# A decoder layer in which the gated MLP's up projection becomes one level of Strassen's product and its down projection is summed in one piece

## The chip, the cores and the metric

The kernel runs on one core of a Trainium2 chip. The metric is the device time of one launch in microseconds. Three runs of the kernel before took 2831.7, 2834.8 and 2835.8 us. One further execution was taken by the hardware profiler, and every row below is from it.

## The reference, cut to what matters

One layer for 512 tokens of width 2048. Three mixers (sparse attention, a state-space scan, block attention) are gated and merged to `m`; the change does not touch them. Then:

```python
x = layer_norm(ALPHA * x + w_out(merged), ln1_g, ln1_b)          # x1, 512 x 2048
u = x1 @ w_up                                                    # 2048 -> 2 x 5632 (gate | value)
u = causal depthwise convolution of width 3 along the tokens, with bias
y = (gelu_tanh(u[:, :5632]) * u[:, 5632:]) @ w_down              # 5632 -> 2048
out = layer_norm(ALPHA * x1 + y, ln2_g, ln2_b)
```

All values are fp32. The kernel writes each operand as a high and a low part, v = h + l, and makes each product from three matmuls: h·h, h·l and l·h.

## The kernel before, in words

**Weights.** Blocks of 128 x 1024 values are loaded by SyncE (SP) into a ring `raw` of three buffers (`pair_unit` for the up projection, `load_raw` for the rest). `split_w` makes the high part `wh` on ScalarE (ACT, line 72) and the low part `wl` on VectorE (DVE, line 73), in rings of two buffers each. The scheduler gives these two a high priority, so in program order they stand early. Every engine works through its own list in order.

**Up projection.** `up_tile(j)`, for j in 0 to 43, takes 128 gate columns and the 128 value columns that go with them. The weights are the stationary operand, the 512 tokens move: 2 x 16 x 3 = 96 matmuls of 512 columns into two PSUM banks. For j = 0 each is cut in two halves of 256 tokens, 192 matmuls. `conv` then reads the bank three times: ACT makes one term (line 947), DVE adds two (line 949). ACT does the gelu, GpSimd (POOL) multiplies gate by value (line 970), and `split` makes `ah` and `al` (lines 83 and 85), which stay in SBUF.

**Down projection.** After every six tiles `down` multiplies the six activation tiles by their rows of `w_down`: four column groups of 512, four token tiles, a PSUM bank each from the side banks `atb` and `avb`. DVE adds each bank to `res` (line 991). The last group is done by `down_last`, token tile by token tile, with LayerNorm 2 behind each.

**LayerNorm 1 and its residual.** `norm_half` normalises two token tiles (line 904), transposes them on TensorE (PE) and applies gain and bias per partition while it writes the high and low parts of x1 (lines 912 to 917). `res` must become ALPHA · x1: `x1_scaled(t)` does this inside the first four up tiles with two POOL operations of 128x2048 (lines 936 and 937) and one ACT operation (line 938).

Of the kernel before, what the change touches and what calls it, by code (L numbers as in the profile page):

```python
# [9 lines left out]
F32 = mybir.dt.float32  # L10
# [21 lines left out]
# gates computed ahead after each part of the mixers  # L32
# [7 lines left out]
def tile_trunk(ctx: ExitStack, tc: tile.TileContext, x, rel_bias, w_in, cq_gain, ckv_gain,  # L40
# [54 lines left out]
    # W as the stationary operand: out[col tile] = W[:, cols]^T @ X^T, 512 tokens wide  # L95
# [16 lines left out]
    # 128 columns at the same place of both halves of a matrix's columns  # L112
# [37 lines left out]
    def s5_pow_e(pool, y, name):  # L150
        # e^y to the last bit or so: y = k ln2 + r, a polynomial in r, 2^k from the exponent bits
# [24 lines left out]
    lhsB = sp.tile([96, 4, 2, 4, P], F32R, name="lhsB")      # h, h, l; q, re/im, G, state  # L176
# [9 lines left out]
    def s5_params():  # L186
# [27 lines left out]
        # sine and cosine by half angles after reduction to [-pi, pi]  # L214
# [28 lines left out]
        # (lam_bar - 1) / lam  # L243
# [22 lines left out]
        # input matrices, block-diagonal over the two groups of a pair, inputs on partitions  # L266
# [27 lines left out]
        # output matrices with the states on partitions  # L294
# [12 lines left out]
        # e^{i theta t}, t < 32  # L307
# [112 lines left out]
    def logits(head, hd, qs, kst, mask):  # L420
        # normalised softmax rows of one head, the four query tiles side by side
# [62 lines left out]
    def u_split(G):  # L484
        # the stacked rows h, l, h of a pair of groups meet h, h, l of its matrices
# [8 lines left out]
    def s5_tile(G):  # L494
# [44 lines left out]
        # 2 gelu(y) in its tanh form  # L539
# [7 lines left out]
    def s5_glu():  # L547
        # 4 times the branch's output: (2 gelu) * (1 + tanh(z/2))
# [24 lines left out]
    def rms_apply(banks, gains, dst, width):  # L573
        # dst = c * gain * (mean(c^2) + eps)^-0.5; the mean token-major, then spread over the partitions
# [25 lines left out]
    def dsa_in():  # L600
# [6 lines left out]
        # index keys on both partition halves; index weights token-major  # L607
# [14 lines left out]
    # value at (p, m) stands for the distance p + 384 - m  # L622
# [26 lines left out]
    def dsa_topk():  # L649
        # exactly the 128 greatest scores of a row, the lower index first among equals  # L650
# [48 lines left out]
    def moba_v(g):  # L699
        # two token tiles share a bank: its flags are cleared once, by the first of them  # L700
# [120 lines left out]
    # merged (gates carried twice the sigmoid)  # L821
# [45 lines left out]

    CH = ((0, 512), (512, 512), (1024, 512), (1536, 256), (1792, 256))
    for c, (c0, n) in enumerate(CH):
        xt = xr.tile([P, NT, n], F32, tag="xt", name="xt")  # L870
        nc.sync.dma_start(xt, x2[:, c0:c0 + n].rearrange("(t p) n -> p t n", p=P))
        kq = 1024 // n
        if c < 4:
            banks = [mm_bank()[:, :n] for _ in range(NT)]
            for k0 in range(0, KD, kq):
                wh, wl = wunit(w_out[0], k0, kq, c0, n)
                for k in range(kq):
                    kk = k0 + k
                    for t in range(NT):
                        tok_mm(banks[t], t, mT[kk][0], mT[kk][1], wh[:, k], wl[:, k], kk == 0, kk == KD - 1)  # L880
# [11 lines left out]
        for ts in ((0,), (1,), (2, 3)):  # L892
            banks = [mm_bank()[:, :n] for _ in ts]
            for kk in range(KD):
                for t, bank in zip(ts, banks):
                    tok_mm(bank, t, mT[kk][0], mT[kk][1], *ws[kk], kk == 0, kk == KD - 1)
            for t, bank in zip(ts, banks):
                residual(t, c, c0, n, xt, bank)
    x1T = [(xp.tile([P, T], F32R, tag="x", name="x1h"), xp.tile([P, T], F32R, tag="x", name="x1l")) for _ in range(KD)]
    def norm_half(hb):  # L900
        hs = slice(256 * hb, 256 * hb + 256)
        for t in (2 * hb, 2 * hb + 1):
            mu, r_ = layer_norm_stats(t, 5)
# [184 lines left out]
```

## Time and profile before

| what | value |
|---|---|
| median of three runs | 2834.8 us (2831.7 to 2835.8) |
| span of the profiled execution | 2832.9 us |
| PE busy with matmuls | 2792.6 us, 99% |
| DVE, ACT, POOL busy | 1449.3, 889.5 and 224.5 us |
| last matmul starts | 2820.4 us |
| granted PE clock, stretch 1408 to 1428 us | 0.66 |

The span runs from the first to the last record of the profiled execution; the profiled execution's own time is this span, 1.9 us below the median of the runs. "Busy" of PE counts pipelined matmuls, so what one matmul costs is read from the distance between the starts of two of them, not from its own duration.

### The profile page before, as it was taken

To read this page: it belongs to the slowest core of one execution; us is meant where nothing else is said; L and a number is where in the kernel's file an instruction comes from. 1 tells how busy PE (TensorE), PEld (TensorE's weight loads), DVE (VectorE), ACT (ScalarE), POOL (GpSimd) and SP (SyncE) were. 2 spreads that over 40 slices of the span, in tenths; PEclk is the share of its full clock that TensorE was granted. 3 is DMA by queue.
4 is the path that set the end of the run, shared out by engine and by line. 5 is a ranking of instruction groups with operands and counts; after the bars stand their busy time and mean duration, and the time that the engine had idled before them with its cause. 6 is when DMAs were issued, how large, how long until landed. Compare 5 with 4: busy or idle time off the path is not lost.

```text
span 2832.9 us, 32264 instructions
## 1 busy us (share of the span) xinstructions
PE 2792.6 (99%) x12651; PEld 2255.8 (80%) x12655; DVE 1449.3 (51%) x2176; ACT 889.5 (31%) x1325; POOL 224.5 (8%) x163
## 2 busy tenths in 40 slices
PE   9999999999999999999899999999999999999998
PEld 7777877777887778889778888888888888888886
DVE  6357988885445446434553334333433333333448
ACT  3243333334344432212532232331322322322321
POOL 0000011110000003100420000000000000000002
PEclk9999999999999999999999999999999999999999
DMA  6223433334332335533433333333333333323333
GB/s 199 84 80 93 127 108 118 117 89 93 82 98 86 96 126 192 168 119 105 134 104 97 97 97 92 99 94 94 97 97 97 97 97 97 97 90 97 97 97 112
DMA packets 352824, 301.82 MB, mean 107 GB/s; under 512 B 20963, under 2 KB 307600, under 8 KB 352160
## 3 DMA queue, kind: packets, MB, share of 16 engines
q1 hardware_dynamic: 339536, 281.44, 33.2%
q10 hardware_dynamic: 10832, 14.12, 1.4%
q0 software_dynamic: 2304, 4.20, 0.6%
q8 instruction: 99, 1.62, 0.2%
q14 instruction: 53, 0.43, 0.0%
HBM read 278.31 MB, written 18.24 MB: 105 GB/s over the span
## 4 chain that ended last, share of the span: by engine, by line
PE 94%; DVE 3%; DMA 1%; issue 1%; POOL 1%; ACT 0%; DVEq 0%; SPq 0%; ACTq 0%; POOLq 0%
PE mmb L91 24%; PE mmb L93 23%; PE mmb L92 23%; PE atb L93 4%; PE atb L92 4%; PE atb L91 4%; PE avb L93 2%; PE avb L91 2%; PE avb L92 2%; PE atb L440 1%; PE atb L642 1%; PE atb L460 1%; PE mmb L711 1%; PE avb L536 1%; PE mmb L712 1%
## 5 line engine op out<-in xcount | busy, mean ns | idle before, releaser
L73 DVE TENSOR_TENSOR wl<-raw,wh 128x1024 fp32r<-128x1024 f32 (+1 forms) x468 | 601.1, 1285 | 946.6 <-ACT wh L72 930.2
L72 ACT ACTIVATE wh<-raw 128x1024 fp32r<-128x1024 f32 (+1 forms) x468 | 489.1, 1045 | 1364.1 <-PE mmb L92 905.0
L91 PE MATMUL mmb<-x1h,wh 128*128 128x512 f32 (+1 forms) x1440 | 552.7, 385 | 5.4 <-ACT wh L72 5.4
L92 PE MATMUL mmb<-x1l,wh 128*128 128x512 f32 (+1 forms) x1440 | 555.5, 386 | 1.6 <-DVE x1l L917 1.6
L93 PE MATMUL mmb<-x1h,wl 128*128 128x512 f32 (+1 forms) x1440 | 526.1, 385 | 6.8 <-DVE wl L73 6.8
L91 PE MATMUL mmb<-xh,wh 128*128 128x512 f32 (+1 forms) x1056 | 419.6, 398 | 1.2 <-ACT wh L72 1.2
L92 PE MATMUL mmb<-xl,wh 128*128 128x512 f32 (+1 forms) x1056 | 418.9, 397 | 0.0
L93 PE MATMUL mmb<-xh,wl 128*128 128x512 f32 (+1 forms) x1056 | 407.5, 397 | 0.6 <-DVE wl L73 0.6
L93 PEld LDWEIGHTS mmb<-x1h,wl 128*128 128x128 f32 x1440 | 270.9, 188 | 61.6 <-DVE wl L73 8.0
L91 PEld LDWEIGHTS mmb<-x1h,wh 128*128 128x128 f32 x1440 | 270.0, 188 | 60.0 <-ACT wh L72 6.3
L92 PEld LDWEIGHTS mmb<-x1l,wh 128*128 128x128 f32 x1440 | 271.3, 188 | 56.8 <-DVE x1l L917 2.6
L91 PEld LDWEIGHTS mmb<-xh,wh 128*128 128x128 f32 (+1 forms) x1056 | 199.3, 189 | 54.7 <-issue 9.0
L93 PEld LDWEIGHTS mmb<-xh,wl 128*128 128x128 f32 (+1 forms) x1056 | 198.7, 188 | 52.7 <-issue 9.4
L92 PEld LDWEIGHTS mmb<-xl,wh 128*128 128x128 f32 (+1 forms) x1056 | 199.1, 189 | 47.4 <-issue 6.9
L93 PE MATMUL atb<-wh,al 128*128 128x512 f32 x480 | 189.8, 395 | 0.0
L92 PE MATMUL atb<-wl,ah 128*128 128x512 f32 x480 | 189.5, 395 | 0.0
L949 DVE SCALAR_TENSOR_TENSOR cv<-mmb,cwc,cv 128x511 f32<-128x511 f32 (+1 forms) x176 | 131.6, 748 | 88.0 <-ACT cv L947 84.8
L91 PE MATMUL atb<-wh,ah 128*128 128x512 f32 x480 | 170.7, 395 | 0.0
L970 POOL TENSOR_TENSOR cv<-cv 128x512 f32<-128x512 f32 x44 | 57.7, 1311 | 1251.7 <-DVE cv L949 1251.7
L93 PEld LDWEIGHTS atb<-wh,al 128*128 128x128 f32 x480 | 89.9, 187 | 22.1
L91 PEld LDWEIGHTS atb<-wh,ah 128*128 128x128 f32 x480 | 90.0, 187 | 21.9
L92 PEld LDWEIGHTS atb<-wl,ah 128*128 128x128 f32 x480 | 90.0, 187 | 21.7
(369 smaller groups left out, 3342.6 us busy)
## 6 DMA issues: line engine op xcount, KB each, us to landing
raw<-in_w_up_dram SPq DMA_DIRECT2D x360, 256.0 KB, 3.4
raw<-in_w_in_dram SPq DMA_DIRECT2D x120, 512.0 KB, 3.7
raw<-in_w_down_dram SPq DMA_DIRECT2D x88, 512.0 KB, 3.6
raw<-in_w_out_dram SPq DMA_DIRECT2D x32, 512.0 KB, 3.7
raw<-in_w_branch_dram SPq DMA_DIRECT2D x24, 512.0 KB, 4.6
thd<-th ACTq DMA_DIRECT2D x22, 512.0 KB, 2.9
th<-thd SPq DMA_DIRECT2D x22, 512.0 KB
raw<-in_w_in_dram SPq DMA_DIRECT2D x32, 256.0 KB, 3.4
```

What stands on the lines that cost most here:

```text
L72: nc.scalar.activation(wh, raw, AF.Copy)
L73: nc.vector.tensor_sub(wl, raw, wh.bitcast(F32))
L91: nc.tensor.matmul(o, ah, bh, start=start, stop=False)
L92: nc.tensor.matmul(o, ah, bl, start=False, stop=False)
L93: nc.tensor.matmul(o, al, bh, start=False, stop=stop)
L440: nc.tensor.matmul(lb[:, :W], s[half, qi], kl[half, :W], start=False, stop=not mk)
L460: nc.tensor.transpose(tb[:, (i - j) * P:(i - j + 1) * P], pt[:, o:o + P], ident)
L536: nc.tensor.matmul(yb[rw], ctr[:, G, rw], t[0], start=True, stop=False, tile_position=(0, 32 * q))
L642: nc.tensor.matmul(lb[:, :W], qs[hd][half, qi], kil[half, :W], start=False, stop=True)
L711: nc.tensor.matmul(o, xh[:, ts_], wl[:, k], start=False, stop=False, skip_group_check=True)
L949: nc.vector.scalar_tensor_tensor(c_[:, s_:], bank[:, :T - s_], cwc[:, j * 88 + f:j * 88 + f + 1], c_[:, s_:], op0=ALU.mult, op1=ALU.add)
L970: nc.gpsimd.tensor_mul(ca, ca, cv)
```

## The change

**Up projection.** The 16 blocks of 128 that the sum runs over are taken as two halves of eight, the tokens as two blocks of 256, and gate and value columns as two column blocks, so one tile is a 2 x 2 block product. Strassen's product in Winograd's form needs seven block products in place of eight. `up_pair(j)` does them in this order on PE: w11·a11, t2·s2, t1·q1, w21·a12, t3·s3, t4·a22, w22·q4. Each is 8 x 3 = 24 matmuls of 256 columns. The token-side operands q1, s2, s3, q4 are built once, after LayerNorm 1. The weight-side sums t1 to t4 are built for each j: t1 and t3 on DVE, t2 and t4 on POOL (`wsum`, line 992), each 128x1024, in a pool `ts` of three buffers. The outputs are put together by DVE in SBUF (`u2`, `u3`, `hf1`, `hf2`, lines 1047 to 1057), and `conv` reads them from SBUF. The first two products of tiles 0 to 3 that need no sums (`pre`, `pre_end`) are done ahead.

**LayerNorm 1.** The last 256 columns of `w_out` are summed in two halves. `norm` applies gain and bias token-major with two DVE operations of 128x1024 for each half row, x1 is stored to DRAM (`resd`), and `turn` transposes 96 blocks, 64 before.

**Activations.** Each tile's product of gate and value is stored to DRAM (`actd`, line 1062, on ACT's queue).

**Down projection.** Two passes of 1024 output columns. In each, all 44 tiles are summed in eight PSUM banks. The activations are loaded again (line 1082, ACT's queue) and split again in each pass. x1 is loaded back (4 MB, line 1077), and `take` adds ALPHA · x1 to the banks at the end of a pass. In the second pass the last eight tiles are held, so that the token tiles end one after the other.

On DVE, a steady up tile before (`wl` is the low part of a weight block, `cv` the convolution, `al` the low part of an activation):

```order
L73 TENSOR_TENSOR wl<-raw,wh 128x1024 x2
L949 SCALAR_TENSOR_TENSOR cv<-mmb,cwc,cv 128x511
L949 SCALAR_TENSOR_TENSOR cv<-mmb,cwc,cv 128x510
L73 TENSOR_TENSOR wl<-raw,wh 128x1024
L949 SCALAR_TENSOR_TENSOR cv<-mmb,cwc,cv 128x511
L949 SCALAR_TENSOR_TENSOR cv<-mmb,cwc,cv 128x510
L73 TENSOR_TENSOR wl<-raw,wh 128x1024
L85 TENSOR_TENSOR al<-cv,ah 128x512
```

On DVE, the middle of a steady up tile of the change, from the split of w21 on (`ts` is t1 or t3, the two after it in a row are t3's and t4's low parts):

```order
L73 TENSOR_TENSOR wl<-raw,wh 128x1024
L992 TENSOR_TENSOR ts<-raw,raw_12905 128x1024
L73 TENSOR_TENSOR wl<-ts,wh 128x1024 x2
L992 TENSOR_TENSOR ts<-raw_12905,raw_12941 128x1024
L1050 TENSOR_TENSOR u_12829<-mmb,p_12671 128x256
L73 TENSOR_TENSOR wl<-raw_12702,wh 128x1024
L1052 TENSOR_TENSOR hf_12831<-mmb,u_12829 128x256
L1055 TENSOR_TENSOR hf_12672<-mmb,u_12829 128x256
L73 TENSOR_TENSOR wl<-raw,wh 128x1024
L1026 SCALAR_TENSOR_TENSOR cv<-hf_12672,cwc,cv 128x511
L1026 SCALAR_TENSOR_TENSOR cv<-hf_12672,cwc,cv 128x510
L1057 TENSOR_TENSOR hf_12831<-mmb,u_12799 128x256
```

Where a tile had four low parts, four convolution steps and one `al`, it now has seven low parts, two sums, five 256-wide operations and four convolution steps, and the convolution reads `hf` in SBUF where it read the bank `mmb`.

On POOL, two steady tiles of the change (`ts` is t2 or t4, `cv` the product of gate and value); before there was the `cv` row alone, line 970, once a tile:

```order
L992 TENSOR_TENSOR ts<-ts,raw_13180 128x1024
L1061 TENSOR_TENSOR cv<-cv 128x512
L992 TENSOR_TENSOR ts<-ts,raw 128x1024
L992 TENSOR_TENSOR ts<-ts,raw_13419 128x1024
L1061 TENSOR_TENSOR cv<-cv 128x512
L992 TENSOR_TENSOR ts<-ts,raw 128x1024
```

Two sums of 128x1024 a tile are new there, one ahead of the product and one behind it.

On ACT, from the last up tile to the first activations of the down projection in the change (`actd` is the store, `af` a load from it):

```order
L72 ACTIVATE wh<-raw 128x1024
L1024 ACTIVATE cv<-hf_21276,c_cb,cwc 128x512
L72 ACTIVATE wh<-raw 128x1024
L1024 ACTIVATE cv<-hf_21435,c_cb,cwc 128x512
L1060 ACTIVATE cv<-cv 128x512
L1062 DMA actd<-cv 128x512
L1082 DMA af<-actd 128x512 x4
L83 ACTIVATE ah<-af 128x512
L1082 DMA af<-actd 128x512
L83 ACTIVATE ah<-af 128x512
L1082 DMA af<-actd 128x512
```

What moved: the loads of all activation tiles stand behind the store of the last one, which waits for POOL's last product.

The core of the diff:

```diff
-    def up_tile(j):
...
-            banks = gemm_pair(wus, j, x1T)
-        ca = conv(banks[0], j)
-        cv = conv(banks[1], 44 + j)
+    def wsum(eng, a, b):
+        t_ = upl.tile([P, 8, P], F32, tag="ts", name="ts", bufs=3)
+        with tc.high_priority(HP):
+            eng.tensor_add(t_, a, b)
+        return t_
+    def prod(bank, src, name, first):
+        wh, wl = hl(src)
+        for k in range(8):
+            xh, xl = X[name, k]
+            for n, (a, b) in enumerate(((wh, xh), (wh, xl), (wl, xh))):
+                nc.tensor.matmul(bank, a[:, k], b, start=first and k == 0 and n == 0,
+                                 stop=k == 7 and n == 2, skip_group_check=True)
...
+    def up_pair(j, done):
+        w11, w12 = wblock(0, 0, j), wblock(0, 1, j)
+        t1 = wsum(nc.vector, w11, w12)
+        st = None if done else pre(j, w11, None)
+        w22 = wblock(1, 1, j)
+        t2 = wsum(nc.gpsimd, t1, w22)
+        B, C = chain_bank(j), chain_bank(j)
+        prod(B, t2, "s2", True)
+        prod(C, t1, "q1", True)
+        w21 = wblock(1, 0, j)
...
+        t3 = wsum(nc.vector, w12, w22)
+        t4 = wsum(nc.gpsimd, t2, w21)
+        nc.vector.tensor_add(u2, B, p1)
+        prod(B, t3, "s3", False)
+        nc.vector.tensor_add(u3, B, p1)
+        nc.vector.tensor_sub(hf2[:, HI], C, u3)
+        prod(Dk, t4, "a22", True)
+        nc.vector.tensor_add(hf1[:, HI], Dk, u3)
+        prod(C, w22, "q4", False)
+        nc.vector.tensor_sub(hf2[:, LO], C, u2)
+        ca = conv(hf1, j)
+        cv = conv(hf2, 44 + j)
         nc.scalar.activation(ca, ca, AF.Gelu_apprx_tanh)
         nc.gpsimd.tensor_mul(ca, ca, cv)
-        h = dp.tile([P, T], F32R, tag="ah", name="ah", bufs=2 * GA)
-        l = dp.tile([P, T], F32R, tag="al", name="al", bufs=2 * GA)
-        split(h, l, ca)
-        return h, l
+        nc.scalar.dma_start(actd[j], ca)
...
-    def x1_scaled(t):
-        nc.gpsimd.tensor_mul(res[:, t], res[:, t], g1b)
-        nc.gpsimd.tensor_add(res[:, t], res[:, t], b1b)
-        nc.scalar.activation(res[:, t], res[:, t], AF.Copy, scale=ALPHA)
...
+    def norm(t, c):
+        nc.vector.scalar_tensor_tensor(y, y, mu, g1b[:, cs_], op0=ALU.subtract, op1=ALU.mult)
+        nc.vector.scalar_tensor_tensor(y, y, r_, b1b[:, cs_], op0=ALU.mult, op1=ALU.add)
+        nc.scalar.dma_start(resd[:, t, cs_], y)
...
+        block("a22", kk, xp, b22)
+        nc.vector.tensor_sub(q1, x21, b22)
+        nc.vector.tensor_sub(s3, b11, x21)
+        nc.vector.tensor_sub(s2, q1, b11)
+        nc.vector.tensor_add(q4, s2, b12)
...
+    y_ = dx.tile([P, NT, D], F32, name="yo")
+    nc.sync.dma_start(y_, resd)
+    for u in range(2):
+        banks = [[mm_bank(), mm_bank()], [mm_bank(), mm_bank()], [at_bank(), at_bank()], [at_bank(), av_bank()]]
+        last = NF if u == 0 else NF - NL
+        for f in range(last):
+            a, w = act_hl(f, False), w_hl(f, u, False)
             for t in range(NT):
-                nc.vector.tensor_add(res[:, t, cs_], res[:, t, cs_], banks[t])
+                down_mm(banks, t, a, w, f)
```

## Rows read from the trace of the kernel before

**Rows 1.** The page: busy time of PE, and the chain that ended last, by engine.

```profile
PE 2792.6 (99%) x12651; PEld 2255.8 (80%) x12655; DVE 1449.3 (51%) x2176; ACT 889.5 (31%) x1325; POOL 224.5 (8%) x163
PE 94%; DVE 3%; DMA 1%; issue 1%; POOL 1%; ACT 0%; DVEq 0%; SPq 0%; ACTq 0%; POOLq 0%
```

**Rows 2.** Timeline of PE: start, duration, instruction; up projection, around 1380 us.

```profile
1379.63 0.39 PE L91 MATMUL mmb<-x1h,wh 128*128 128x512 f32 x1
...
1380.31 0.39 PE L91 MATMUL mmb<-x1h,wh 128*128 128x512 f32 x1
1380.53 0.28 PE L92 MATMUL mmb<-x1l,wh 128*128 128x256 f32 x1
...
1380.89 0.28 PE L93 MATMUL mmb<-x1h,wl 128*128 128x256 f32 x1
```

**Rows 3.** Timeline of PE: 24 matmuls in a row at the end of the down projection.

```profile
2814.99 0.39 PE L91 MATMUL atb<-dwh,ah 128*128 128x512 f32 x1
...
2820.36 0.39 PE L93 MATMUL avb<-dwh,al 128*128 128x512 f32 x1
```

**Rows 4.** Windows: busy time by engine (instructions), granted PE clock, DMA share, GB/s.

```profile
1000.00:1100.00 100.00, 99.22 (x436) 81.83 (x437) 51.28 (x51) 25.60 (x30) 19.43 (x15) 1.00 0.48 156
1181.00:1290.00 109.00, 109.00 (x482) 90.25 (x481) 34.23 (x36) 21.22 (x20) 0.00 (x0) 1.00 0.37 119
1381.00:1428.00 47.00, 34.80 (x139) 27.16 (x138) 26.49 (x16) 18.55 (x18) 42.65 (x9) 0.85 0.37 120
```

**Rows 5.** Waits, 1381 to 1428 us: total us, times, longest.

```profile
ACT res L938 <- POOL res L937: 14.0, 3, 9.6
DVE al L85 <- ACT ah L83: 10.0, 1, 10.0
PE mmb L93 <- DVE wl L73: 6.8, 2, 6.2
```

**Rows 6.** Timeline of POOL, DVE and PE, 1396 to 1429 us; x2 joins neighbours.

```profile
1396.25 11.16 POOL L936 TENSOR_TENSOR res<-res,bc 128x2048 f32<-128x2048 f32 x2
1398.87 1.53 DVE L949 SCALAR_TENSOR_TENSOR cv<-mmb,cwc,cv 128x511 f32<-128x511 f32 x2 [1.48 <-ACT cv L947]
...
1413.15 9.43 POOL L937 TENSOR_TENSOR res<-res,bc 128x2048 f32<-128x2048 f32 x2
1414.44 3.77 DVE L85 TENSOR_TENSOR al<-cv,ah 128x512 fp32r<-128x512 f32 x1 [10.05 <-ACT ah L83]
1417.63 10.45 POOL L937 TENSOR_TENSOR res<-res,bc 128x2048 f32<-128x2048 f32 x2
1418.14 5.53 DVE L73 TENSOR_TENSOR wl<-raw,wh 128x1024 fp32r<-128x1024 f32 x1
```

**Rows 7.** Groups by shape, five steady up tiles, 2180 to 2290 us.

```profile
L73 DVE TENSOR_TENSOR wl<-raw,wh 128x1024 fp32r<-128x1024 f32 x20 | 24.5, 1226 | 56.9 <-ACT wh L72 56.9
L72 ACT ACTIVATE wh<-raw 128x1024 fp32r<-128x1024 f32 x20 | 21.2, 1061 | 63.5 <-PE mmb L92 63.5
L949 DVE SCALAR_TENSOR_TENSOR cv<-mmb,cwc,cv 128x511 f32<-128x511 f32 x10 | 7.5, 747 | 9.5 <-ACT cv L947 9.5
L970 POOL TENSOR_TENSOR cv<-cv 128x512 f32<-128x512 f32 x5 | 6.4, 1288 | 169.6 <-DVE cv L949 169.6
L85 DVE TENSOR_TENSOR al<-cv,ah 128x512 fp32r<-128x512 f32 x5 | 3.4, 684 | 0.0
```

**Rows 8.** Groups by shape, 1319 to 1385 us: DVE around LayerNorm 1; PE, 1343 to 1382.

```profile
L917 DVE TENSOR_TENSOR x1l<-x,x1h 128x256 fp32r<-128x256 f32 x32 | 12.7, 421 | 4.5 <-ACT x L916 3.9
...
L92 PE MATMUL mmb<-x1l,wh 128*128 128x256 f32 x64 | 19.1, 309 | 1.6 <-DVE x1l L917 1.6
```

**Rows 9.** DMA issues: KB each, median us from issue to landing.

```profile
raw<-in_w_up_dram SPq DMA_DIRECT2D x360, 256.0 KB, 3.4
...
thd<-th ACTq DMA_DIRECT2D x22, 512.0 KB, 2.9
...
bc<-in_ln_b_dram SPq DMA_DIRECT2D x2, 1024.0 KB, 9.1
```

More of the change, by code (lines that the diff above doesn't have):

```diff
@@ L939, in tile_trunk @@
[L939 to L947 removed]
+        for t in range(NT):
+            for kk in range(KD // 2, KD):
+                tok_mm(banks[t], t, mT[kk][0], mT[kk][1], *ws[kk - KD // 2], False, kk == KD - 1)
+            residual(t, c, c0, n, xt, banks[t])
@@ new lines, in tile_trunk, with turn, block @@
+    for t in range(NT):
+        mvs[t] = layer_norm_stats(t, 5)
+        for c in range(2):
+            norm(t, c)
+    def turn(i0, hb, kk):
+        tb = av_bank() if (i0, hb) == (0, 1) else at_bank()
+        for k in range(2):
+            for i in range(2):
+                c0 = (8 * hb + 2 * kk + k) * P
+                nc.tensor.transpose(tb[:, (2 * k + i) * P:(2 * k + i + 1) * P], res[:, i0 + i, c0:c0 + P], ident)
+        return tb
+    X = {}
+    def block(name, kk, pool, src):
+        h = pool.tile([P, 512], F32R, tag="x", name="x1h")
+        l = pool.tile([P, 512], F32R, tag="x", name="x1l")
+        split(h, l, src)
+        for k in range(2):
+            X[name, 2 * kk + k] = (h[:, 256 * k:256 * k + 256], l[:, 256 * k:256 * k + 256])
@@ new lines, in tile_trunk @@
+    with tc.high_priority(100):
+        for kk in range(4):
+            block("a11", kk, xq1, turn(0, 0, kk))
+        for kk in range(4):
+            block("a12", kk, xq1, turn(0, 1, kk))
+    lx.close()
+    ux = ExitStack()
+    xq2 = right(ux, "xq2", 8)
+    upp = right(ux, "upp")
+    tmx = ExitStack()
+    tmp2 = right(tmx, "tmp2", 6)
+    for kk in range(4):
+        b21, b22, b11, b12 = turn(2, 0, kk), turn(2, 1, kk), turn(0, 0, kk), turn(0, 1, kk)
+        f = [tmp2.tile([P, 512], F32, tag="tm", name="tm") for _ in range(5)]
+        x21, q1, s2, s3, q4 = f
+        nc.scalar.activation(x21, b21, AF.Copy)
+        block("a22", kk, xp, b22)
[3 more added lines that the diff above has]
+        nc.vector.tensor_add(q4, s2, b12)
+        block("q1", kk, xp, q1)
+        block("s2", kk, xp, s2)
+        block("s3", kk, xp, s3)
+        block("q4", kk, xq2, q4)
@@ L1030, in tile_trunk @@
-    waiting = None
-    for gi, grp in enumerate(groups):
-        acts = []
-        for j in grp:
-            acts.append(up_tile(j))
-            if j < NT:
-                x1_scaled(j)
-        if gi >= len(groups) - 2 and waiting is None:
-            waiting = grp, acts
-            continue
-        if waiting:
-            down(*waiting)
-            down_last(grp, acts)
-        else:
-            down(grp, acts)
+        nc.scalar.dma_start(actd[j], ca)
+    done = {}
+    for j in range(NPRE):
+        w11, w21 = wblock(0, 0, j), wblock(1, 0, j)
+        done[j] = pre_end(pre(j, w11, w21))
@@ new lines, in tile_trunk, with act_hl @@
+    for j in range(NF):
+        up_pair(j, done.get(j))
+    ux.close()
+    NL = 8
+    wd = w_down[0]
+    dx = ctx.enter_context(tc.tile_pool(name="dx", bufs=1, reuse_waits="tile"))
+    y_ = dx.tile([P, NT, D], F32, name="yo")
+    nc.sync.dma_start(y_, resd)
+    g2b, b2b = bcast(dx, ln2_g[0], "g2b"), bcast(dx, ln2_b[0], "b2b")
+    def act_hl(f, held):
+        raw = dx.tile([P, T], F32, tag="af", name="af", bufs=4)
+        nc.scalar.dma_start(raw, actd[f])
+        if held:
+            h = xq1.tile([P, T], F32R, tag="x", name="ah")
+            l = xq1.tile([P, T], F32R, tag="x", name="al")
+        else:
+            h = dx.tile([P, T], F32R, tag="ah", name="ah", bufs=3)
+            l = dx.tile([P, T], F32R, tag="al", name="al", bufs=3)
+        with tc.high_priority(HP):
+            split(h, l, raw)
+        return h, l
@@ new lines, in down_mm, with take @@
+    def down_mm(banks, t, a, w, f):
+        ts_ = slice(t * P, (t + 1) * P)
+        for n, (x_, m_) in enumerate(((0, 0), (0, 1), (1, 0))):
+            for c in range(2):
+                nc.tensor.matmul(banks[t][c], a[x_][:, ts_], w[c][m_],
+                                 start=f == 0 and n == 0, stop=f == NF - 1 and n == 2)
+    def take(t, u, banks):
+        for c in range(2):
+            cs_ = slice(1024 * u + 512 * c, 1024 * u + 512 * c + 512)
+            nc.vector.scalar_tensor_tensor(y_[:, t, cs_], y_[:, t, cs_], ALPHA, banks[t][c], op0=ALU.mult, op1=ALU.add)
+        for c in range(2):
+            cs_ = slice(1024 * u + 512 * c, 1024 * u + 512 * c + 512)
+            nc.vector.bn_stats(stats[:, t, 2 * u + c], y_[:, t, cs_])
```

228 lines of the change are left out of this document (112 added, 116 removed).

## The prediction, as put on record before the changed kernel ran

> **What bounds the kernel now.** I read the page first. PE is busy 99% of the span and 94% of the chain that ended last [rows 1], so a matmul not issued is time saved, unless something else stops PE. Two questions are left: what one matmul costs, and which engine PE would wait for.
>
> The cost is the distance between starts. In the timeline of the up projection four matmuls of 512 columns start 0.68 us apart from first to last of three steps, 0.2267 each; three steps of 256 columns take 0.36, 0.120 each [rows 2]. So a 256-column matmul costs 0.529 of a 512-column one, not half. At the end of the down projection 23 steps of 512 columns take 5.37 us, 0.2335 each [rows 3]. The output projection, which has the same form (weights move, tokens stand), ran 482 in 109 us, 0.226 [rows 4].
>
> Then the one long stop. From 1381 to 1428 us PE issued 139 matmuls, worth 139 x 0.2267 = 31.5 us, in 47 us at a granted clock of 0.85 [rows 4]: 15.5 us lost. The waits there say how: ACT waits for POOL's `x1_scaled` 14.0 us, DVE's `al` stands behind ACT 10.0 us, and PE waits for `wl` [rows 5]. The timeline shows a second thing. While POOL worked at 128x2048, a `wl` that takes 1.23 us took 5.53, and an `al` that takes 0.68 took 3.77 [rows 6, 7]; each ended about its own length after a POOL operation had ended. A two-input SBUF operation of DVE and one of POOL run one after the other. The convolution steps, which read PSUM, took 0.76 beside POOL [rows 6], as alone (0.75, [rows 7]).
>
> **What the change takes away.**
>
> (a) Matmuls. Before: 43 x 96 x 0.2267 + 192 x 0.120 = 958.8 us. After: 44 x 7 x 24 = 7392 x 0.120 = 887.0. −71.8. (One eighth would be 120; the dearer column eats 48.)
>
> (b) `x1_scaled` and its stop: −15.5.
>
> (c) The rate of the down projection. 2112 matmuls stay 2112. Its slower 0.2335 is seen with the side banks and the activation pool of before; the new passes use all banks and other pools. I cannot show the cause. At the output projection's rate (I take 0.2267) it is −14.4, at worst 0. I take −14, and give it 0.7.
>
> Sum: −101.3.
>
> **What it adds.**
>
> (d) LayerNorm 1 to the first sum. After the first token tile's statistics DVE has 16 operations of 128x1024 for gain and bias (1.23 each by `wl`, 19.6), 28 low parts of 512 (0.684, 19.1), 16 sums and differences of 512 (0.68, 10.9), some six low parts of weights (7.4), and about 5 of small ones: 62 us, 56 if neighbours overlap by 0.1 each. Behind it comes t1, t2, high part, low part: 1.23 + 2.35 + 1.06 + 1.23 = 5.9. PE has only 42 us to set beside it (rest of the output projection 9, 96 transposes of about 0.11, eight products of 24 x 0.120 = 23). Idle 20 to 26, I take 24; before it was some 2.6 (1.6 of it in [rows 8]). +21.4, and 32 more transposes, +3.5.
>
> (e) The steady tile. PE's work is 7 x 2.88 = 20.16 us, against 21.76 before. DVE's is nine operations of 1.23, four convolution steps of 0.75 and five of 0.42 [rows 7, 8], 16.2; POOL's is two sums and a product. The sum of 1024 is not in the trace: between 512 (1.29, [rows 7]) and 2048 (4.48, the distance of two starts in [rows 6]) it comes to 2.35. So POOL has 6.0. If these exclude each other, 13.9 of DVE's (all but the five that read PSUM) and POOL's 6.0 fill 19.9 of 20.16. It would fit only without holes, and there is an order to keep: with two buffers a weight block is split while the one before it is multiplied, so each slot of 2.88 holds 0.08 + 1.06 (`wh`) + 0.03 + 1.23 (`wl`), 2.40, and `wl` is first read by the third matmul, 0.24 later. Slack 0.72. A POOL sum that has just begun when `wl` is ready makes it up to 2.35 − 0.72 = 1.63 late, the product 1.29 − 0.72 = 0.57.
>
> I walked one tile by hand in the program's order, each row at its duration, from the start of w21·a12. t1 for the next tile ends at 1.3, and t2 starts only after the low part of t3 (2.5) has freed its buffer: 2.5 to 4.9. The low part of t4 could start at 4.1, runs 4.9 to 6.0 and is just in time for its third matmul. The convolutions end at 15.3, POOL's product runs 15.4 to 16.7, in the way of the low part of the next t1, which ends 17.8: PE waits 0.3. t4 needs that same low part out of its buffer, runs 17.9 to 20.2, across the low part of w21 (ready at 18.5, done 21.35): PE waits 0.7. Tile: 21.15. With a sum of 2.2 it is 20.9, with 2.6 21.6. Bounds: 20.16 without exclusion, 20.16 + 2 x 1.63 + 0.57 = 24.0 with every collision at its worst. I take 21.2: 40 tiles x 1.04 = +41.6.
>
> The Trainium skill says the same of the pair of engines (SBUF — State Buffer, "Who interferes with whom"): a DVE instruction with two SBUF inputs and a GpSimd instruction that reads SBUF hold a shared port pair as a lock, and a DVE instruction with at most one SBUF input does not contend. The trace agrees, with 5.53 for 1.23 on the one side and 0.76 for 0.75 on the other. By it the convolution, moved from PSUM to `hf` in SBUF, joins the locked ones; had it stayed outside, 13.9 would be 10.9.
>
> (f) Tiles 0 to 3 have five products each, 14.4 us of PE, but the same 19.9 of DVE and POOL less two low parts: t4 comes late. About 17.1 each, +10.8.
>
> (g) The seam to the down projection. All loads of activations stand on ACT behind the store of tile 43, which waits for POOL's last product. After PE's last matmul: combination 0.4, ACT's term 0.6, two convolution steps 1.4, product 1.3, store issue, load 2.9 (the 512 KB store in [rows 9]), two halves of a split 1.3: 8 to 9 us with nothing for PE, perhaps 14 if the clock falls as it did around the stop above. I take 11. Then 4 MB of x1 and 2 MB of gains pass on SP between the fifth and the sixth weight block; 1 MB took 9.1 [rows 9], the ring of three covers part: 0 to 8, I take 3. The switch of passes, where DVE drains eight banks: 1.5. Tail after the last matmul: 12.5 before, the same operations now, +0.5.
>
> The loads do not bind otherwise. A tile asks 2 MB in 21 us, 100 GB/s, the down passes 768 KB in 5.4 us, 141; 156 were moved at PE's full pace elsewhere [rows 4].
>
> Sum: 21.4 + 3.5 + 41.6 + 10.8 + 11 + 3 + 1.5 + 0.5 = +93.3. Net −8.0: a span of 2824.9 for 2832.9, and with the 1.9 us by which the median of the runs lies above the profiled one, **2827 us**, 0.3% less. It is a small difference of two large sums, and one microsecond a tile is 40 us.
>
> **Rivals.**
>
> *POOL fits into the gaps.* DVE idles 4 us a tile; if t4 falls there, or the sums run faster than 2.35, tiles take 20.2 to 20.4, worth −32 to −40 more: about 2790. For it: 19.9 of 20.16 fits on paper. Against: the order of DVE's list leaves `wl` only 0.72 of slack. It decides below 20.9 a tile.
>
> *The lock takes more than it gives* (slower). If each of the two sums stops a low part for one full length less slack, not one of them as in my walk, a tile is 20.16 + 1.63 + 0.7 + 0.3 = 22.8, longer than the 21.76 of before: +64, about 2890; half of that, one more late `wl` of 0.8 a tile, gives 22.0 and 2859. For it: in [rows 6] POOL and DVE alternate, both late. Against: t2 starts right after a low part, with the next one 1.6 us away. It decides from 21.4 a tile on, where the net is zero.
>
> *The down projection keeps 0.2335* (and all else as taken): 2841, slower by 0.2%.
>
> *The matmul rate of the skill.* If 256 columns cost just over half of 512 here, (a) would be −118 and the kernel faster by another 46 or so, near 2781. The starts in [rows 2] speak against it; 0.05, within the 0.23 below. In the Trainium skill (TensorE: Matmul & The Clock Gate, "Back-to-back issue gap") an isolated gap is 262 cycles for 256 columns and 518 for 512, 109 and 216 ns by an estimate at 2.4 GHz; the rows have 120 and 227.
>
> **How the numbers follow.** The runs of before lie within 2831.7 and 2835.8, so 0.2% (5.7 us) is about what can be told from no change. Chances: as walked, 2800 to 2850, 0.45 (0.25 of it below 2829, 0.10 within 0.2%, 0.10 above 2840); POOL fits or the rate is better, 2775 to 2800, 0.23; lock dearer, 2850 to 2890, 0.22; the down rate alone unchanged, 0.10, half of it within 0.2%. Faster: 0.23 + 0.25 = 0.48; same 0.10 + 0.05 = 0.15; slower 0.10 + 0.22 + 0.05 = 0.37. Range 2780 to 2872, which leaves out the outer halves of the two wings; the likeliest case's own range is 2800 to 2850.
>
> **What the profile after would show.** (a) matmul starts 0.120 apart within a product. (c) 0.227 in the down passes. (d) PE idle between 1345 and 1400 waiting for DVE, some 24 us. (e) tiles of 21.2 with PE waiting for `wl` at line 73, twice a tile, and `wl` means well above 1.23; steady tiles of 20.2 or 22 make me wrong. (g) one stop of 8 to 14 us ahead of the first down matmul, waiting for ACT or DVE behind a load. The prediction fails if the collision of POOL's sums with `wl` is not some 1 us a tile, or if an idle stretch lowers the granted clock for long.

## The result, and the profile after

The changed kernel takes 2862.9 us (median of four runs, 2856.6 to 2865.1) against 2834.0 for the kernel before (four runs, 2831.7 to 2835.8): ratio 1.0099, 95% interval 1.0084 to 1.0113. It is 1% slower, where 0.3% faster was forecast. The time lies inside the stated range, on the other side of zero.

The page of the changed kernel, its span, its busy times and the chain that ended last by engine:

```profile
span 2863.3 us, 39514 instructions
PE 2741.4 (96%) x15757; PEld 2362.5 (83%) x15757; DVE 1851.8 (65%) x2550; ACT 1058.3 (37%) x1565; POOL 440.2 (15%) x243
PE 34%; DVE 12%; ACT 3%; issue 1%; DMA 0%; DVEq 0%; ACTq 0%; POOL 0%; POOLq 0%
```

PE has 51 us less to do than in [rows 1], and the span is 30 us longer. The chain could be followed back through half of the span only (its shares add up to 50%), and DVE has 12% in that half, where it had 3% of the whole: PE now waits for it. The windows of the stages (busy time by engine with instructions, granted PE clock, DMA share, GB/s) say where:

```profile
1345.00:1400.00 55.00, 39.71 (x290) 36.55 (x291) 50.05 (x68) 27.72 (x48) 6.29 (x3) 0.86 0.52 163
1400.00:1475.00 75.00, 63.28 (x470) 61.00 (x469) 63.47 (x61) 28.24 (x30) 29.18 (x11) 0.93 0.39 115
1600.00:2300.00 700.00, 662.91 (x5396) 649.93 (x5395) 570.71 (x578) 317.33 (x385) 225.33 (x97) 1.00 0.37 109
2345.00:2400.00 55.00, 35.28 (x158) 29.38 (x157) 16.67 (x22) 13.97 (x18) 1.26 (x1) 0.78 0.64 229
2400.00:2600.00 200.00, 200.00 (x884) 165.68 (x883) 70.19 (x73) 57.42 (x73) 0.00 (x0) 1.00 0.46 146
```

PE stands still for 15 us around LayerNorm 1 (first row), for 37 of 700 us in the steady tiles (third), and for 20 around the seam to the down projection (fourth). In the down passes it is never idle. PE's own waits from 1300 us to the end, in total us, times and longest:

```profile
PE mmb L1000 <- DVE wl L73: 40.5, 49, 1.2
PE mmb L1114 <- ACT ah L83: 19.7, 1, 19.7
PE mmb L1000 <- DVE hf L1052: 17.4, 43, 2.3
PE mmb L1000 <- ACT wh L72: 10.0, 3, 9.1
```

The first and third are the tiles, once each in nearly every one. The second is one single wait of 19.7 us: the seam. The fourth is LayerNorm 1.

A steady tile takes 21.80 us from one w11 to the next. From the starts of its seven products: 2.88, 2.88, 2.88, 4.02, 2.88, 3.38, 2.88. Five run at the 0.120 us of [rows 2]; w21·a12 is 1.14 too long, and 0.50 is lost ahead of w22·q4. The timeline of POOL, DVE and PE in one tile (start, duration, instruction, idle time before it and what ended it) shows both:

```profile
1807.95 2.27 POOL L1061 TENSOR_TENSOR cv<-cv 128x512 f32<-128x512 f32 x1 [11.34 <-DVE cv L1026]
1810.18 2.40 POOL L992 TENSOR_TENSOR ts<-ts,raw 128x1024 f32<-128x1024 f32 x1
1810.72 2.94 DVE L73 TENSOR_TENSOR wl<-raw,wh 128x1024 fp32r<-128x1024 f32 x1 [0.48 <-ACT wh L72]
1813.71 0.38 PE L1000 MATMUL mmb<-x1h,wl 128*128 128x256 f32 x1 [0.89 <-DVE wl L73]
...
1816.01 2.41 POOL L992 TENSOR_TENSOR ts<-ts,raw 128x1024 f32<-128x1024 f32 x1 [3.43 <-DVE wl L73]
1817.67 1.83 DVE L73 TENSOR_TENSOR wl<-ts,wh 128x1024 fp32r<-128x1024 f32 x1 [1.74 <-ACT wh L72]
1819.53 1.22 DVE L992 TENSOR_TENSOR ts<-raw,raw 128x1024 f32<-128x1024 f32 x1
1821.01 1.21 DVE L73 TENSOR_TENSOR wl<-raw,wh 128x1024 fp32r<-128x1024 f32 x1
1822.14 0.41 DVE L1052 TENSOR_TENSOR hf<-mmb,u 128x256 f32<-128x256 f32 x1
1822.70 0.36 PE L1000 MATMUL mmb<-x1h,wh 128*128 128x256 f32 x1 [0.26 <-DVE hf L1052]
```

POOL's t4 runs from 1810.18 to 1812.58. The low part of w21, ready at 1810.72, ends at 1813.66, 1.1 us after t4, and PE goes on at 1813.71. Then t2 (1816.01) stretches the low part of t4's product from 1.23 to 1.83; DVE's list behind it is late by that much, and its last entry, `hf` of line 1052, reads the bank C at 1822.14, into which w22·q4 is to be added. PE may not write the bank before it is read. The groups by shape of the stretch 1600 to 2200 us give the means:

```profile
L73 DVE TENSOR_TENSOR wl<-raw,wh 128x1024 fp32r<-128x1024 f32 x83 | 148.0, 1783 | 28.3 <-ACT wh L72 28.3
L73 DVE TENSOR_TENSOR wl<-ts,wh 128x1024 fp32r<-128x1024 f32 x110 | 151.3, 1375 | 60.4 <-ACT wh L72 59.6
L992 POOL TENSOR_TENSOR ts<-ts,raw 128x1024 f32<-128x1024 f32 x55 | 132.2, 2403 | 96.1 <-DVE wl L73 96.1
L1061 POOL TENSOR_TENSOR cv<-cv 128x512 f32<-128x512 f32 x27 | 61.2, 2265 | 306.4 <-DVE cv L1026 306.4
```

Low parts that took 1226 ns in [rows 7] take 1783 and 1375, and POOL's product 2265 for 1288. Each side waits for the other.

### The profile page after: what moved, and what is told of

It is laid out like the page before. It is cut to its first block, busy times and chain, and to the rows that moved or that the text cites. A ratio compares the mean times of both kernels' runs of the same rounds, so it can differ in the third digit from the quotient of the medians.

```text
span 2863.3 us, 39514 instructions
## 1 busy us (share of the span) xinstructions
PE 2741.4 (96%) x15757; PEld 2362.5 (83%) x15757; DVE 1851.8 (65%) x2550; ACT 1058.3 (37%) x1565; POOL 440.2 (15%) x243
## 4 chain that ended last, share of the span: by engine, by line
PE 34%; DVE 12%; ACT 3%; issue 1%; DMA 0%; DVEq 0%; ACTq 0%; POOL 0%; POOLq 0%
PE mmb L1000 17%; DVE wl L73 9%; PE mmb L1114 8%; PE atb L1114 6%; ACT wh L72 3%; DVE ts L992 2%; PE avb L1114 2%; DVE hf L1052 1%; DVE u L1050 1%; DMA af<-actd 0%; DVE cv L1026 0%; DVE yo L1139 0%; DVEq L1198 0%; DVE yo L1138 0%; DVE yo L1120 0%
## 5 line engine op out<-in xcount | busy, mean ns | idle before, releaser
L73 DVE TENSOR_TENSOR wl<-raw,wh 128x1024 fp32r<-128x1024 f32 (+2 forms) x422 | 603.2, 1430 | 330.4 <-ACT wh L72 309.3
L1000 PE MATMUL mmb<-x1h,wl 128*128 128x256 f32 x2464 | 707.9, 287 | 40.7 <-DVE wl L73 40.5
L1000 PE MATMUL mmb<-x1h,wh 128*128 128x256 f32 x2464 | 703.7, 286 | 27.9 <-DVE hf L1052 17.4
L72 ACT ACTIVATE wh<-raw 128x1024 fp32r<-128x1024 f32 (+2 forms) x422 | 438.9, 1040 | 730.0 <-PE mmb L92 358.6
L1000 PE MATMUL mmb<-x1l,wh 128*128 128x256 f32 x2464 | 699.4, 284 | 0.0
L1000 PEld LDWEIGHTS mmb<-x1h,wl 128*128 128x128 f32 x2464 | 473.9, 192 | 52.1 <-DVE wl L73 50.9
L1000 PEld LDWEIGHTS mmb<-x1h,wh 128*128 128x128 f32 x2464 | 474.4, 193 | 37.0 <-issue 25.2
L1000 PEld LDWEIGHTS mmb<-x1l,wh 128*128 128x128 f32 x2464 | 474.5, 193 | 0.0
L73 DVE TENSOR_TENSOR wl<-ts,wh 128x1024 fp32r<-128x1024 f32 x176 | 240.5, 1367 | 94.4 <-ACT wh L72 93.3
L992 POOL TENSOR_TENSOR ts<-ts,raw 128x1024 f32<-128x1024 f32 x88 | 215.9, 2453 | 211.5 <-DVE wl L73 136.6
```

Of the source, the lines that this page charges most:

```text
L72: nc.scalar.activation(wh, raw, AF.Copy)
L73: nc.vector.tensor_sub(wl, raw, wh.bitcast(F32))
L992: eng.tensor_add(t_, a, b)
L1000: nc.tensor.matmul(bank, a[:, k], b, start=first and k == 0 and n == 0, stop=k == 7 and n == 2, skip_group_check=True)
```

## The experiments

The theory (A): POOL's operations that read SBUF keep DVE's two-input operations waiting for their whole length, and DVE's list carries the delay to PE in two places; the seam is a separate stop made by the 4 MB load. The rival (B): DVE and POOL simply have too much work for a tile of 20.16 us, wherever it is put; and the loads at the seam are slow by themselves. All times are medians, ratios to runs of the kernel before made beside them; tile times and stops are distances between matmul starts.

**POOL's sums in pieces (e1_pieces).**

```diff
-            eng.tensor_add(t_, a, b)
+            if eng is nc.gpsimd:
+                for q in range(0, 8, 2):
+                    eng.tensor_add(t_[:, q:q + 2], a[:, q:q + 2], b[:, q:q + 2])
+            else:
+                eng.tensor_add(t_, a, b)
```

> Edit: each POOL sum (t2, t4) is done in four pieces of 128x256 instead of one of 128x1024; nothing else. Theory A (a POOL instruction holds DVE off for its whole length): the low part of w21, 2.94 us in the changed kernel because it waits for t4, waits at most one piece of some 0.7 us, so the stop of PE ahead of it (1.05 us a tile) falls to 0 to 0.2, the stop of 0.42 ahead of w22's product stays; a steady tile goes from 21.8 to 20.6 to 20.9 us and the kernel from 2863 to 2815 to 2827. Theory B (DVE and POOL together simply have too much work for a tile, in whatever pieces): the tile stays at 21.8 or grows, since the pieces add fixed time; 2860 to 2880.

Measured: 2833.8 us, ratio 0.9995 (0.9986 to 1.0005), 29 us less than the changed kernel; tile 21.24. Above the 2815 to 2827 of A, below B's 2860. The product of w21 is back at 2.88 and the wait ahead of w22 is down from 0.50 to about 0.07, but a stop of 0.99 has appeared in t3's product, ahead of its low part. The groups of 1600 to 2200 us:

```profile
L994 POOL TENSOR_TENSOR ts<-ts,raw 128x256 f32<-128x256 f32 x224 | 268.5, 1230 | 69.2 <-DVE wl L73 69.2
L73 DVE TENSOR_TENSOR wl<-raw,wh 128x1024 fp32r<-128x1024 f32 x84 | 106.5, 1268 | 30.7 <-ACT wh L72 28.9
L996 DVE TENSOR_TENSOR ts<-raw,raw 128x1024 f32<-128x1024 f32 x56 | 80.3, 1435 | 57.8 <-POOL ts L994 56.8
```

The low parts of `raw` blocks are down from 1783 to 1268. But a piece takes 0.74 alone and 1.72 when it meets a DVE operation, so t4 is finished later, and DVE's next t1, which needs a `ts` buffer that t4 reads, waits 57 us in 28 tiles for it; t3's low part stands behind that t1 in DVE's list. The mechanism is A's; the price, that POOL too is held off, was not in my expectation.

**All sums on DVE (e2_dve).**

```diff
-        t2 = wsum(nc.gpsimd, t1, w22)
+        t2 = wsum(nc.vector, t1, w22)
...
-        t4 = wsum(nc.gpsimd, t2, w21)
+        t4 = wsum(nc.vector, t2, w21)
```

> Edit: t2 and t4 are summed by DVE, POOL keeps only the product of gate and value. Theory A: the low parts of weights take 1.23 again except where the product of 1.3 us meets them; DVE has 18.7 us of work in 20.16, and an operation of 1.23 ahead of a low part costs up to 0.5; a tile of 20.8 to 21.4, kernel 2822 to 2847. Theory B (too much work on DVE is the cause): DVE becomes the bound, tile at or above 21.8, kernel 2863 to 2890.

Measured: 2798.5 us, ratio 0.9875 (0.9858 to 0.9891), tile 20.42. Better than A's interval, and far from B's: with more work on the engine that PE waits for, 1.39 us a tile went away. In the groups of 1600 to 2200 us all low parts are back at their old length (1219 ns for those of `raw`, 1221 for those of `ts`), and what is left of the collision is on t2:

```profile
L73 DVE TENSOR_TENSOR wl<-raw,wh 128x1024 fp32r<-128x1024 f32 x89 | 108.5, 1219 | 18.5 <-ACT wh L72 16.6
L992 DVE TENSOR_TENSOR ts<-ts,raw 128x1024 f32<-128x1024 f32 x58 | 99.5, 1716 | 2.0
L1061 POOL TENSOR_TENSOR cv<-cv 128x512 f32<-128x512 f32 x29 | 63.9, 2203 | 528.1 <-ACT wh L72 528.1
```

**Bank C read early (e3_copyc).**

```diff
         prod(C, t1, "q1", True)
+        cc = upl.tile([P, 256], F32, tag="cc", name="cc", bufs=2)
+        nc.scalar.activation(cc, C, AF.Copy)
...
-        nc.vector.tensor_sub(hf2[:, HI], C, u3)
+        nc.vector.tensor_sub(hf2[:, HI], cc, u3)
```

> Edit: ACT copies the bank C after the product t1*q1, and hf2's upper half is made from the copy, so that w22's product need not wait until DVE has read C. Theory A (the 0.42 us stop a tile ahead of w22's product is the wait for DVE's read of its own bank, behind two 1.23 us operations): the stop goes, 40 x 0.42 = 17 us less, 2845 to 2850. Theory B (the matmuls wait for the low part of w22 or for DVE anyway): the stop stays or moves, 2860 to 2866.

Measured: 2837.9 us, ratio 1.0008 (0.9999 to 1.0018), 25 us less than the changed kernel, more than A's 17. The product ahead of w22 is at 2.95 for 3.38, the one of w21 unchanged at 4.03; a tile 21.33. PE's wait for line 1052 is gone from the list. The rest of the gain is in tiles 0 to 3, 71.0 us for 78.4, where the same wait had been up to 2.3 us long.

**x1's load later, first try (e4_seam).**

```diff
-    nc.sync.dma_start(y_, resd)
-    g2b, b2b = bcast(dx, ln2_g[0], "g2b"), bcast(dx, ln2_b[0], "b2b")
...
+            if u == 0 and f == 12:
+                nc.sync.dma_start(y_, resd)
+            if u == 0 and f == 24:
+                gb = [bcast(dx, ln2_g[0], "g2b"), bcast(dx, ln2_b[0], "b2b")]
```

> Edit: x1 (4 MB) is loaded back ahead of the 13th weight block of the down projection's first pass and the two gains ahead of the 25th, instead of all at its start. Theory A (the stop of 19.7 us ahead of the down projection is the first activation load queued behind the 4 MB: 13.5 us against 2.6 for a load alone): the stop falls to 8 to 9.5 us and the kernel to 2849 to 2853. Theory B (the load is slow because it follows its own store, or by ACT's queue): the stop stays near 19 us, 2860 to 2866. Cost on the other side: a later 4 MB could hold weight blocks back by up to 8 us in the middle of the pass.

Measured: 2866.5 us, ratio 1.0111 (1.0096 to 1.0126), as the changed kernel. The edit did not do what it says: SP issued the loads at 2348.2 to 2349.1 us, ahead of all activation loads, now 6 MB in a row. The stop grew from 20.0 to 25.1 us. The first activation load was issued only at 2363.6, 14.0 us behind the store of tile 43, and landed 5.0 later; what held its issue is not shown. The run does not decide between A and B.

**x1's load later, tied to its place (e5_seam2).** As e4_seam, with the load queued by an explicit edge behind the weight block just issued:

```diff
+            if u == 0 and f == 12:
+                with tc.issue_after(wq[-1].ins):
+                    nc.sync.dma_start(y_, resd)
```

> Edit: as the changed kernel, but x1's 4 MB are queued on SP behind the 13th weight block of the first down pass and the two gains behind the 25th (in e4_seam the scheduler had put them ahead of the activations again, now 6 MB in a row, and the stop grew from 20.0 to 25.1 us). Theory A (the first activation load waits behind those megabytes): the stop falls to 8 to 9.5 us, the kernel by 10 to 14 to about 2851. Theory B (a load behind its own store is slow by itself): stop still near 19, 2862 to 2867. In the middle of the pass the 4 MB may cost 0 to 8 us.

Measured: 2853.6 us, ratio 1.0063 (1.0048 to 1.0078), 9 us less than the changed kernel; the stop is 10.9 us for 20.0. A's mechanism, a little less than its 10 to 14. DMA issues of the changed kernel in 2345 to 2375 us and of this one in 2350 to 2400 (KB each, median us to landing):

```profile
yo<-resd SPq DMA_DIRECT2D x1, 4096.0 KB
...
af<-actd ACTq DMA_DIRECT2D x6, 256.0 KB, 10.1
```

```profile
af<-actd ACTq DMA_DIRECT2D x14, 256.0 KB, 2.8
raw<-in_w_down_dram SPq DMA_DIRECT2D x6, 512.0 KB, 3.7
```

In the changed kernel the first activation load took 13.5 us to land, with the 4 MB under way and the DMA engines 99% busy (next row, columns as in the windows above); here it took 2.7, though the store of tile 43 stands ahead of it as before, so B is out.

```profile
2356.00:2360.00 4.00, 0.00 (x0) 0.00 (x0) 0.00 (x0) 0.00 (x0) 0.00 (x0) 0.50 0.99 389
```

ACT's wait for `af` is 16.8 us in one piece in the changed kernel (first row), 7.7 at most here (second):

```profile
ACT ah L83 <- DMA af<-actd: 16.8, 1, 16.8
```

```profile
ACT ah L83 <- DMA af<-actd: 8.7, 2, 7.7
```

**Both (e6_dve_seam2).** The edits of e2_dve and e5_seam2 together.

> Edit: both e2_dve (all four sums on DVE) and e5_seam2. If the two costs are independent, as theory A has them (one is in the tiles, the other between the stages): 2798.5 less the 10 to 14 us of e5_seam2, 2785 to 2789, faster than both kernels by 1.5 to 1.8%. If one hides the other: above 2793.

Measured: 2790.8 us, ratio 0.984 (0.9824 to 0.9856), between the two forecasts. Tile 20.42, stop 10.9: each cost as in its own run. The total is 8 us below e2_dve, not 10 to 14; tiles 0 to 3 took 74.1 us here and 69.1 there. POOL's product of tile 0 shows what differs, here (first row) and in e2_dve (second); the third row is ACT's wait here, 1415 to 1435 us:

```profile
1418.90 6.60 POOL L1061 TENSOR_TENSOR cv<-cv 128x512 f32<-128x512 f32 x1 [62.90 <-ACT wh L72]
1418.03 2.06 POOL L1061 TENSOR_TENSOR cv<-cv 128x512 f32<-128x512 f32 x1 [62.82 <-ACT wh L72]
ACT wh L72 <- POOL cv L1061: 7.1, 1, 7.1
```

In e2_dve POOL got its turn behind one low part of DVE. Here it was held through five two-input operations in a row, until DVE read a bank at 1424.27. The product's store stands on ACT ahead of the next high part, which waited 7.1 us, and PE stopped behind it. Tile 2 has a second product of 6.66. What decides who comes first is not shown: in both runs the product began 0.3 us after a low part of DVE.

**The price of `x1_scaled` (e7_no_scaled).** In the kernel before:

```diff
-            if j < NT:
-                x1_scaled(j)
```

> Edit: the kernel before without x1_scaled (the residual of the MLP then is the normalised x1 without gain, bias and ALPHA). It prices the stop that the change removes. Theory A (PE lost 15.5 us around these POOL operations): 2817 to 2821. Theory B (part of that time comes back elsewhere, since the weight ring had run ahead): 2824 to 2835.

Measured: 2821.7 us, ratio 0.995 (0.9935 to 0.9965), 13.9 less; the forecast of term (b) was 15.5. That is 0.7 above A's interval and below B's. The window that held 139 matmuls at a clock of 0.85 in [rows 4]:

```profile
1381.00:1428.00 47.00, 45.28 (x201) 36.91 (x200) 20.78 (x23) 17.77 (x21) 3.55 (x3) 1.00 0.57 181
```

**No products ahead (e8_npre0).**

```diff
-    NPRE = 4
+    NPRE = 0
```

> Edit: as the changed kernel with NPRE = 0, so that no product is done ahead of the sums and all 44 tiles are alike. Theory A (the 55 us between the output projection and the first sum are DVE's work on LayerNorm 1 and the operands, and the eight products lie beside it): the stretch falls only by the eight weight splits that DVE no longer has in it, to 43 to 50 us, and tiles 0 to 3 go from 19.6 to 21.8, +9: 2860 to 2868. Theory B (PE's own work fills that stretch): it falls by the 23 us of products, and the kernel by some 14, to 2848 to 2852.

Measured: 2865.2 us, ratio 1.0102 (1.0087 to 1.0117), as the changed kernel. The first product with a sum starts 45.9 us after the last matmul of the output projection, for 55.4: 9.5 us shorter, as A had it. DVE was busy 44.4 of the 47 us from 1343, PE 24.0 at a granted clock of 0.68. Doing products ahead hides 23 us of PE's work but adds their splits to the engine that sets the end.

**Activations 32 bytes off (e9_phase).**

```diff
+    pad = dx.tile([P, 8], F32, name="pad")
+    nc.gpsimd.memset(pad, 0.0)
     def act_hl(f, held):
```

> Edit: as the changed kernel, with an unused 32-byte tile in front of the activation buffers of the down projection, so that their addresses are 32 bytes off the weights' (mod 64), as they were in the kernel before; nothing else. Theory A (the 0.2335 of before comes from where the stationary operand starts): the 1920 matmuls that read these buffers go from 0.227 to 0.233 each, +12 to 13 us, 2873 to 2878; the 192 on the held tiles stay. Theory B (banks or the order of matmuls made it): no change, 2861 to 2866.

Measured: 2875.0 us, ratio 1.0141 (1.0126 to 1.0156), 12.1 more than the changed kernel. The window 2400 to 2600 us, where the changed kernel had 884 matmuls:

```profile
2400.00:2600.00 200.00, 200.00 (x858) 161.00 (x858) 69.02 (x72) 57.02 (x72) 0.00 (x0) 1.00 0.46 141
```

The mean distance of starts over 1700 matmuls is 0.2333 here and 0.2267 there; on the held tiles, whose place did not move, 0.2267 in both. Banks and order are the same in the two kernels, so the place of these buffers makes the rate, as A says. That the buffers of the kernel before stood so is the premise of the run; no trace shows an address.

**POOL with idle additions, and with fills (e10_pool_add, e11_pool_memset).** On e2_dve, whose low parts are undisturbed:

```diff
-        nc.gpsimd.tensor_mul(ca, ca, cv)
+        mul = nc.gpsimd.tensor_mul(ca, ca, cv)
+        with tc.issue_after(mul.ins):
+            for _ in range(2):
+                nc.gpsimd.tensor_add(sc, sc, sc)
```

In e11_pool_memset the last two lines are:

```diff
+            for _ in range(4):
+                nc.gpsimd.memset(sc, 0.0)
```

> Edit: e2_dve (all sums on DVE, tile 20.42 us) with two idle POOL additions of 128x1024 into a scratch tile queued behind each product of gate and value; nothing waits for them. Theory A (a POOL operation that reads SBUF holds off DVE's operations with two SBUF inputs): DVE's low parts take up to 3.6 us where they meet them, a tile grows by 0.8 to 2.5 us, the kernel to 2830 to 2900. Theory B (POOL costs only by what waits for its results): tile 20.4, 2795 to 2802.

> Edit: as e10_pool_add, but POOL fills the scratch tile four times (128x1024 memsets, which write SBUF and read nothing) in place of the two additions. Theory A, in its form that only POOL's reads collide with DVE's second input: tile stays at 20.4, 2795 to 2802. Theory A in a wider form (any POOL operation on SBUF): a tile grows as with the additions, in proportion to POOL's time. Theory B: no change either.

Measured: with additions 2895.4 us, ratio 1.0211 (1.0194 to 1.0228), tile 22.88, which is 2.46 more than e2_dve for work whose result nobody reads. With fills 2791.0, ratio 0.9841 (0.9826 to 0.9855), tile 20.42 as in e2_dve (the difference to its 2798.5 is mainly at the seam: x1's load was issued 3.6 us behind the first activation load, and the stop was 9.6 for 20.5 us). Groups of 1600 to 2200 us, additions first:

```profile
L1064 POOL TENSOR_TENSOR sc<-sc 128x1024 f32<-128x1024 f32 x52 | 146.5, 2817 | 2.0
L73 DVE TENSOR_TENSOR wl<-raw,wh 128x1024 fp32r<-128x1024 f32 x79 | 131.9, 1670 | 14.4 <-ACT wh L72 14.4
```

```profile
L1064 POOL MEMSET sc<- 128x1024 f32 x116 | 110.7, 954 | 5.0
L73 DVE TENSOR_TENSOR wl<-raw,wh 128x1024 fp32r<-128x1024 f32 x89 | 108.5, 1220 | 18.4 <-ACT wh L72 16.6
```

B's form "POOL costs only by what waits for it" is out. The narrow form of A holds: POOL's reads collide, its fills do not, though they were 3.8 us a tile: 29 of the 89 low parts in the last row lie beside a fill for over 0.3 us, and these take 1.21. That is the rule of the Trainium skill cited in the prediction (SBUF — State Buffer, "Who interferes with whom"), which holds of GpSimd instructions that read SBUF and not of those that only write it; the runs agree, with 1670 against 1220 ns.

**Nothing on POOL (e12_no_pool).** e6_dve_seam2 with the product on DVE:

```diff
-        nc.gpsimd.tensor_mul(ca, ca, cv)
+        nc.vector.tensor_mul(ca, ca, cv)
```

> Edit: e6_dve_seam2 with the product of gate and value on DVE too, so that POOL has no work in the up tiles. Theory A (the 0.26 us a tile that are left in e2_dve and e6_dve_seam2 come from t2's sum waiting for POOL's product): DVE gains 0.7 us of work and loses the wait, a tile of 20.2 to 20.35, the kernel 2782 to 2788. Theory B (DVE is now simply full, 19.3 of 20.16): a tile of 20.4 to 20.9, 2790 to 2810.

Measured: 2774.1 us, ratio 0.9783 (0.9768 to 0.9797), tile 20.16, better than A's interval. It is the fastest kernel of this study, 2.2% below the kernel before and 89 us below the changed one. Its window of 600 us in the tiles:

```profile
1600.00:2200.00 600.00, 600.00 (x5003) 599.53 (x5002) 548.43 (x627) 294.77 (x358) 0.00 (x0) 1.00 0.41 119
```

PE has no idle time at all, beside a DVE that is busy 548 of 600 us. DVE has 0.7 us more to do in each tile than in e2_dve, and the tile is 0.26 shorter.

## Why the prediction was wrong, point by point

The forecast span was 2824.9, the measured one 2863.3, 38 us more. By its own terms:

- **(a) Matmuls: right.** 0.120 a matmul, 2.88 a product wherever nothing stops PE.
- **(b) `x1_scaled`: right**, 13.9 for 15.5 (e7_no_scaled).
- **(c) Rate of the down projection: right**, but as a bet at 0.7, with no cause known. e9_phase shows a cause that makes the 0.2333: where the stationary operand starts.
- **(d) LayerNorm 1: right.** 55.4 us from the last matmul of the output projection to the first product with a sum; the forecast was 24 idle with 10.6 of transposes and 23 of products, 57.6. The parts were off and nearly cancel, which is luck: PE stood for 17.0 and was busy for 38.4, at a mean granted clock of 0.88, between its levels of 1.2 and 2.4 GHz. e8_npre0 shows that DVE sets its end.
- **(e) The steady tile: the step that failed.** 21.8 for 21.2, 40 times, +24 us: this alone turns the sign. The collision of POOL with the low parts is the mechanism that was named, and nearly of the size that was named. In the walk by hand PE lost 0.3 ahead of the low part of t1's product and 0.7 ahead of w21's, 1.0 together; measured are 0 and 1.14: the low part of t1 came first, POOL's product waited for it (2.27 for 1.29), and t4 began only behind the product and held up w21's low part for 1.86 of its 2.40 us. What failed is a wait that the walk put at nothing: it let w22·q4 start when its weights were ready. It left out that the bank C must first be read by `hf` of line 1052, at the end of a list of DVE that a collision has made late: 0.50 a tile, 20 of the 24 us, shown by e3_copyc. In e2_dve nothing reads C early, and the wait is gone too: with undisturbed low parts DVE gets there in time.
- **(f) Tiles 0 to 3: mis-sized.** 78.4 us for 68.4, +10, by the same two kinds of wait: PE stood 7.3 us for `hf` of line 1052, up to 2.3 at a time, and 4.3 for low parts. e12_no_pool, with nothing on POOL, takes the 68.4, so the forecast priced these tiles as if nothing collided.
- **(g) The seam: mis-sized in one term.** Stop 20.0 us, where 11 was forecast and 3 more for x1's 4 MB somewhere later, +6 in all. I had put the 4 MB behind the fifth weight block, as the program's order shows, and overlooked that SP reaches that point before ACT issues the first activation load: the issue of the 4 MB is at 2352.4, that of the first load at 2354.2, and its data were used at 2367.7. The DMA engines were 99% busy from 2352 to 2364. e5_seam2 takes 9 us of it away. After the stop, in which PE did nothing, the first 14 down matmuls start some 0.43 us apart, at a granted clock of 0.50 (1.2 GHz), as the forecast feared: 2.9 us.

The remaining terms (end of the output projection, (d), pass switch, tail, clock) come to about −1.5 together.

Three sums of the prediction are off, without moving the forecast. Nine operations of 1.23 and four of 0.75 make 14.1, not 13.9. At 262 and 518 cycles (a) would be −110, not −118, and that rival 2789. 768 KB in 5.4 us are 146 GB/s, not 141; the down passes moved 146. That the convolution joins the locked operations is not shown either way: its steps took 0.75 as before, and none ran beside a POOL operation.

The rival that came true in size lies between the likeliest case and "the lock takes more than it gives": it was to decide from 21.4 a tile on, and the tile was 21.8. My argument against it was that t2 starts 1.6 us ahead of the next low part. It did, 1816.01 against 1817.67, and made that low part 0.6 late, in time for its own matmuls as walked. I stopped following it there; the 0.6 went on through t3, u3 and the low part of w22 to the read of C. That the time is near this rival's half case (one more late `wl`, 22.0 a tile, 2859) is in part chance: the late low part cost by the read of C, and 16 us of the total come from (f) and (g).

## What to carry to other kernels

Work moved to an engine that has time to spare is not free if that engine shares a way to memory with the one on the path: 4.8 us of additions on an 85% idle POOL cost more than the same additions on the busiest engine after PE. When a tile is walked by hand, every write into a bank needs the last read of it in the list, and each collision has to be charged to both sides. A load that nobody needs for hundreds of microseconds should be tied to its place in the queue; the place in the source text is not one.

## What was not expected of the hardware

- A stationary operand that starts 32 bytes off costs 3% of a 512-column matmul, 0.2333 for 0.2267 us (e9_phase), with the same banks and order. One offset was tried.
- POOL is held off as well: a piece of 128x256 takes 0.74 us alone and 1.72 when it meets a DVE operation of 1.23 (e1_pieces), so cutting its work small protects DVE and delays POOL. A product that takes 1.29 alone was once held for 6.60, through five DVE operations in a row (e6_dve_seam2).
- POOL's fills of SBUF (0.95 us each, four a tile) leave DVE's low parts at 1220 ns; its additions make those of `raw` blocks 1670 (e10_pool_add, e11_pool_memset).
